# Weight transfers issued by POOL instead of the common queue, and POOL's small fills on VectorE, in a hybrid attention and mLSTM encoder layer

## Chip, cores and metric

One core of a Trainium2 chip runs the whole program. The metric is the device time of one execution in microseconds. Engines: PE is TensorE, DVE is VectorE, ACT is ScalarE, POOL is GpSimd, SP is SyncE. SP computes nothing in this kernel; it only issues transfers.

## What is computed

```python
def _encoder_layer(h, ...):                     # h: 16 meta tokens + sequence, 1024 wide
    xn = _rmsnorm(h, g_pre)
    proj = xn @ w_in + b_in                     # 1024 x 6672
    na_q, na_k, na_v, na_z, ml_qk, ml_v, ml_z, ml_o, ml_g, mg = jnp.split(proj, SPLIT_IDX, axis=-1)
    ya = _neighbourhood_attention(na_q, na_k, na_v, na_rpb)    # 8 heads of 64, window 8 x 16 on a grid 64 wide
    ya = (ya * jax.nn.silu(na_z)) @ w_a
    yb = (_mlstm_branch(ml_qk, ml_v, ml_g, ml_o, ml_conv_w, ml_head_g) * jax.nn.silu(ml_z)) @ w_b
    ga, gb = jnp.split(jax.nn.sigmoid(mg), 2, axis=-1)
    y = (ga * ya + gb * yb) @ w_out
    return h + _rmsnorm(y, g_post)
```

This is done once for a sequence of 1024 tokens (s = 0) and once for one of 2048 (s = 1), all in float32. The mLSTM branch has 4 heads of 128 and runs in both directions in chunks.

## The kernel before

Every float32 product is made of three products of a faster type: an operand x is split into `hi` (rounded) and `lo` (the rest), and `hi*hi + hi*lo + lo*hi` is added up in PSUM (`mm3`, lines 143 to 146, and the same by hand at 394 to 396 and 1284 to 1286).

Two generators run interleaved. `dense` makes the projections: `group` (input projections of 1024 tokens, by feature in `fm_half` and by token in `tm_unit`), then `final` for six blocks of 512 tokens. In `final` the first half multiplies `w_a` and `w_b` in 8 feature tiles (L144 to L146, with `yh`, `yl`); VectorE multiplies each result with a gate tile `tg` (L1263), adds the two branches (L1265) and splits them (L1266, L1267). The second half multiplies `w_out` in four column blocks (L1284 to L1286). `sparse` makes the mLSTM (`ml`, `ml_norm`) and neighbourhood attention (`na`) stages: scores (L644, L645), softmax (L648 to L661), transposition (L669) and splitting (L671, L672) of the weights, and the product with the values (L681). `run` takes from `dense` as much work as `sparse` has announced in us.

TensorE's order is written out by that interleaving. The order of all other engines, SP's and POOL's queues among them, is made by a scheduler when the program is built; each engine then works through its list in that order, so that an instruction that waits holds up all that follow on its engine. All transfers but 14 stand in SP's list.

The weights pass through `wload` and `wpump`. The first time that a tile of weights is used, it is loaded raw (`wraw`, L215), ScalarE makes `whi` (L233), POOL (the first three) or VectorE makes `wlo` (L236), and both are stored to memory (`wh`, `wl`, L240). Each later time they are loaded back from there (L231). Of `whi` and `wlo` there are four buffers each (`NBW = 4`); `wdone` is called where the last product of a tile has been issued to TensorE, and it pumps the next one:

```python
    def wdone(self, n=1):
        self.wout -= n
        self.wpump()
```

The gate tiles are loaded two feature tiles ahead, from four buffers (L1247):

```python
                    tg = fp.tile([P, n], F32, name="tg", tag="stT", bufs=4)
                    nc.sync.dma_start(tg, self.GT[s][8 * br + ft][:, t0:t0 + n])
```

POOL has little: the first three `wlo`, small fills of constants (`ss` L276, `km` L341 with two copies L342 and L343, `gt` L543 and L544, `g_t` L704 and L705, `g_mp` L760, `raw` L820 and L822, `va` L856 and L857, `st` L952), and the 14 transfers of `qB` (L541) and `kx` (L617) for attention.

Of the kernel before, what the change touches and what calls it, by code (L numbers as in the profile page):

```python
# [9 lines left out]
F32 = mybir.dt.float32  # L10
# [11 lines left out]
NM = 16  # L22
# [88 lines left out]
class K:  # L111
# [107 lines left out]
    def wpump(self):  # L219


        nc, wp = self.nc, self.wp
        self.wload()
        while self.wraw and self.wout < NBW:
            key, raw, nk, w = self.wraw.popleft()
            n = nk * w
            hi = wp.tile([P, 4 * WU], F32R, name="whi", bufs=NBW)
            lo = wp.tile([P, 4 * WU], F32R, name="wlo", bufs=NBW)
            if raw is None:
                for x, d in zip((hi, lo), self.wkept[key]):  # L230
                    nc.sync.dma_start(x[:, :n].bitcast(F32), d[:, :])  # L231
            else:
                nc.scalar.activation(hi[:, :n], raw[:, :n], AF.Copy)  # L233
                self.nu += 1
                eng = nc.vector if self.nu > 4 else nc.gpsimd
                eng.tensor_tensor(lo[:, :n], raw[:, :n], hi[:, :n].bitcast(F32), op=ALU.subtract)  # L236
                self.wkept[key] = []
                for x, part in ((hi, "h"), (lo, "l")):
                    d = self.dp.tile([P, n], F32, name=f"w{part}{len(self.wkept)}")
                    nc.sync.dma_start(d[:, :], x[:, :n].bitcast(F32))  # L240
                    self.wkept[key].append(d)
            self.wrdy.append([x[:, :n].rearrange("p (k c) -> p k c", k=nk) for x in (hi, lo)])
            self.wout += 1
            self.wload()
# [10 lines left out]
    def build_half(self, s, t0, meta, res, tags=("pj",), xp=None, per=4):  # L255

        nc, wp = self.nc, self.wp
        src = self.i["x_prompt" if s == 0 else "x_sample"]
        base = NM if meta else 0
        jobs = [(src[t0 + P * j:t0 + P * (j + 1), :], P, base + P * j) for j in range(4)]  # L260
        js = [jobs[a:a + per] for a in range(0, 4, per)]
        if meta:
            js[-1] = js[-1] + [(self.i["meta"], NM, 0)]
        xh = xl = None
        cnt = 0
        scaled = []
        for grp in js:
            xs = []
            for ap, n, col in grp:
                xr = (xp or wp).tile([P, D], F32, name="xr", bufs=5 if xp else 4)  # L270
                nc.sync.dma_start(xr[:n], ap)
                xs.append((xr, n, col))
            yield
            m = len(grp)
            ss = wp.tile([P, 5], F32, name="ss", bufs=2)
            nc.gpsimd.memset(ss, 1.0)  # L276
            for q, (xr, n, _) in enumerate(xs):
                junk = wp.tile([P, D], mybir.dt.bfloat16, name="xsq", tag="thT", bufs=1)
                nc.scalar.activation(junk[:n], xr[:n], AF.Square, accum_out=ss[:n, q:q + 1])
                yield  # L280
            nc.vector.tensor_scalar(ss[:, :m], ss[:, :m], 1.0 / D, EPS, op0=ALU.mult, op1=ALU.add)
            r = self.rsqrt8(wp, ss[:, :m], [P, m])
            yield
            for q, (xr, n, col) in enumerate(xs):
                nc.vector.scalar_tensor_tensor(xr[:n], xr[:n], r[:n, q:q + 1], self.gpre[:n], op0=ALU.mult, op1=ALU.mult)
                yield
            yield "scaled"
            if xh is None:
                xh = wp.tile([P, KT, HALF], F32R, name="xh", bufs=2)
                xl = wp.tile([P, KT, HALF], F32R, name="xl", bufs=2)  # L290
            for xr, n, col in xs:
                for e in range(2):
                    pt = self.psum(tags[cnt % len(tags)], [P, 4, P])
                    cnt += 1
                    for j in range(4):
                        nc.tensor.transpose(pt[:, j, :n], xr[:n, (4 * e + j) * P:(4 * e + j + 1) * P], self.ident[:n, :n])
                    h = xh[:, 4 * e:4 * e + 4, col:col + n]
                    nc.scalar.activation(h, pt[:, :, :n], AF.Copy)
                    nc.vector.tensor_tensor(xl[:, 4 * e:4 * e + 4, col:col + n], pt[:, :, :n], h.bitcast(F32), op=ALU.subtract)  # L299
                    yield  # L300
        res.append((xh, xl))


    def fm_evac(self, col, s, t0, meta, chunks, ps):

        nc, wp = self.nc, self.wp
        bi = (col // P) if col < 4608 else 36 + (col - 4624) // P
        bias = self.bfm[:, bi:bi + 1]
        st = wp.tile([P, HALF], F32, name="st", bufs=4)
        m = NM if meta else 0  # L310
        n = 512 + m
        for (c0, c1), p in zip(chunks, ps):
            o, q = st[:, c0:c1], p[:, :c1 - c0]
            if col < C_NK:
                nc.scalar.activation(o.rearrange("p (b r c) -> p r b c", r=8, b=4), q.rearrange("p (r b c) -> p r b c", r=8, b=4),
                                     AF.Identity, bias=self.bq8[:, bi:bi + 1], scale=0.125)
            elif C_NZ <= col < C_MQ:
                zb = wp.tile([P, HALF], F32, name="st", bufs=4)
                nc.scalar.activation(zb[:, c0:c1], q, AF.Identity, bias=bias)
                nc.scalar.activation(o, q, AF.Tanh, bias=self.bfh[:, bi:bi + 1], scale=0.5)  # L320
                nc.vector.scalar_tensor_tensor(o, o, 1.0, zb[:, c0:c1], op0=ALU.add, op1=ALU.mult)
            elif col >= C_GA:
                nc.scalar.activation(o, q, AF.Tanh, bias=self.bfh[:, bi:bi + 1], scale=0.5)
            else:
                nc.scalar.activation(o, q, AF.Identity, bias=bias)
        if C_MQ <= col < C_MV:
            dst = (self.MQ if col < C_MK else self.MK)
            h = (col % 512) // P
            lo = 0 if meta else NM + t0
            nc.sync.dma_start(dst[s][h][:, lo:lo + n], st[:, :n])  # L330
            if meta:
                nc.sync.dma_start(dst[1 - s][h][:, :NM], st[:, :NM])
            return
        if col >= C_GA:
            dst = self.GT[s][(col - C_GA) // P]
        else:
            dst = (self.NQ, self.NK, None, self.NZ)[col // 512][s][(col % 512) // P]
        nc.sync.dma_start(dst[:, t0:t0 + 512], st[:, m:n])
        if meta and C_NK <= col < C_NV:
            km = wp.tile([P, 64], F32, name="km", bufs=1)  # L340
            nc.gpsimd.memset(km, 0.0)  # L341
            nc.gpsimd.tensor_copy(km[:, 8:24], st[:, :NM])  # L342
            nc.gpsimd.tensor_copy(km[:, 32:48], st[:, :NM])  # L343
            nc.sync.dma_start(self.NKM[(col % 512) // P][:, :], km)

    def fm_half(self, col, w, x, s, t0, meta, done=None):
# [185 lines left out]
    def na(self, s, rts):  # L532
# [3 lines left out]
        with tc.tile_pool(name=f"na{s}{rts[0]}", bufs=1, side="right", reuse_waits="tile") as np_:  # L536
# [3 lines left out]
            for q in self.qB:  # L540
                nc.gpsimd.dma_start(q[64:128], i["onehot"].rearrange("a (b c) -> a b c", b=4))  # L541
            for g in self.gts:
                nc.gpsimd.memset(g[:, 0, :], 0.0)  # L543
                nc.gpsimd.memset(g[:, 16, :], 0.0)  # L544
            heads = [(rt, pr, hh) for rt in rts for pr in range(4) for hh in range(2)]
            n = len(heads)
            prep = self.na_prep(np_, s, rows, heads, 0)
# [147 lines left out]
    def ml_gates(self, s, keep, mp, res):  # L695
# [5 lines left out]
        kt = lambda n: keep.tile([P, NC_, 4], F32, name=n, bufs=1)  # L701
        gt = t("g_t", [P, NC_, 16])
        for d in range(2):
            nc.gpsimd.memset(gt[:, 0, 8 * d:8 * d + 4], -BIG)  # L704
            nc.gpsimd.memset(gt[:, 0, 8 * d + 4:8 * d + 8], 1.0e4)  # L705
        nc.sync.dma_start(gt[:NM, 0, :], self.GA[s][0:NM, :])
        nc.sync.dma_start(gt[:, 1:, :], self.GA[s][NM:, :].rearrange("(c p) g -> p c g", p=P))
        yield 3.0
# [21 lines left out]
        def one(d):  # L730
# [26 lines left out]
            nc.vector.tensor_tensor(ra, px[0:1, :NR], rg, op=ALU.add)  # L757
            me = t("g_me", [1, NR], bufs=2)
            mpv = t("g_mp", [1, NR], bufs=2)
            nc.gpsimd.memset(mpv, 0.0)  # L760
            yield
            for h in range(4):
                w = slice(h, NR, 4)
# [49 lines left out]
    def conv_load(self, mp, src, c0, n, T):  # L813

        nc = self.nc
        L = NM + T
        raw = mp.tile([P, BL + 2], F32, name="raw", bufs=3)
        a, b = max(c0 - 1, 0), min(c0 + n + 1, L)
        if a > c0 - 1:
            nc.gpsimd.memset(raw[:, 0:1], 0.0)  # L820
        if b < c0 + n + 1:
            nc.gpsimd.memset(raw[:, n + 1:n + 2], 0.0)  # L822
        nc.sync.dma_start(raw[:, a - c0 + 1:b - c0 + 1], src[:, a:b])
        return raw

# [14 lines left out]
    def ml(self, s):  # L840
# [3 lines left out]
        with tc.tile_pool(name=f"mg{s}", bufs=1, side="right", reuse_waits="tile") as keep:  # L844
# [8 lines left out]
            with tc.tile_pool(name=f"ml{s}", bufs=1, side="right", reuse_waits="tile") as mp:  # L853
                self.vas = [mp.tile([P, CB, 130], F32, name=f"va{j}") for j in range(3)]
                for va in self.vas:
                    nc.gpsimd.memset(va[:, :, 128:129], 1.0)  # L856
                    nc.gpsimd.memset(va[:, :, 129:130], 0.0)  # L857
                for h in range(4):
                    sts = {}
                    yield from self.ml_states(mp, s, h, g, NB, sts)  # L860
# [12 lines left out]
    def ml_states(self, mp, s, h, g, NB, sts):  # L873
# [51 lines left out]
        for i in range(N):  # L925
# [23 lines left out]
            b = (c0 - NM) // BL  # L949
            if b == NB - 1:  # L950
                sts[b] = mp.tile([P, CB, 260], F32, name="st", bufs=NB)
                nc.gpsimd.memset(sts[b][:, CB - 1, 130:260], 0.0)  # L952
            if b:
                sts[b - 1] = mp.tile([P, CB, 260], F32, name="st", bufs=NB)
            for j in range(CB - 1, -1, -1):
# [513 lines left out]
```

## Time and profile before

| | |
|---|---|
| median of 3 runs | 2958.22 us (2955.35 to 2959.94) |
| profiled execution | 2951.54 us, span 2949.8 us, granted clock 0.991 |
| PE, PEld | 2837.0 us (96%), 2520.4 us (85%) |
| DVE, ACT, POOL | 1788.2 us (61%), 1322.5 us (45%), 23.5 us (1%) |
| transfers | 633.33 MB, mean 215 GB/s; queue q1 (SP) 627.46 MB, queue q0 (POOL) 2.69 MB |

The profile is of one execution. A line such as `DVE tg L1263 <- DMA tg<-gt: 30.6, 21, 4.3` in a list of waits says that VectorE's instructions of line 1263 that write `tg` waited 30.6 us in total, 21 times and 4.3 us at most, for the transfer into `tg`. `SPq` is SP's queue of issues. In a list of groups the columns are line, engine, operation, tile written and tiles read, shapes and count; then busy us and mean ns of one; then the engine's idle time before them and what ended it. A row of the chain or of a timeline has start and length in us. The idle time of an engine that is not the bottleneck costs nothing.

### The profile page before, as it was taken

Reading aid. Unit: us, or ns where it says so; the run is one execution under the profiler, and the core shown is the slowest. Engines: PE = TensorE matmul, PEld = TensorE weight load, DVE = VectorE, ACT = ScalarE, POOL = GpSimd, SP = SyncE. Lnnn points to the kernel's source line nnn. Section 1 sums busy time; section 2 is a strip of 40 time slices with the busy share of each in tenths; the row PEclk is TensorE's granted clock in tenths of the full one; section 3 lists DMA queues with packets and bytes.
Section 4 is the critical chain, followed back from the end, with each engine's and each line's share of the span. In section 5 each row is a group of like instructions: output and inputs, shape, how many; then the busy total and the mean of one; then the engine's idle time right before and its main releaser. Section 6 shows DMA issues by size and latency. Waiting matters only on the chain. (4 is left out here: it accounts for less than half of the span.)

```text
span 2949.8 us, 49769 instructions
## 1 busy us (share of the span) xinstructions
PE 2837.0 (96%) x17616; PEld 2520.4 (85%) x17616; DVE 1788.2 (61%) x4818; ACT 1322.5 (45%) x3178; POOL 23.5 (1%) x111
## 2 busy tenths in 40 slices
PE   6999999999999999999999999999999989999998
PEld 6998897899799988888888988877887978888897
DVE  5233566556656764565566565495568877776853
ACT  4113545433443453455565454434455544544421
POOL 1000000000000000000000000000000000000000
PEclk9999999999999999999999999999999999999999
DMA  7555666556756563666765554496579898988875
GB/s 252 199 176 183 204 212 204 166 176 210 237 176 197 152 189 101 203 193 194 222 206 189 173 182 151 160 356 196 179 232 329 288 276 268 281 273 252 287 260 205
DMA packets 415914, 633.33 MB, mean 215 GB/s; under 512 B 51920, under 2 KB 252704, under 8 KB 415664
## 3 DMA queue, kind: packets, MB, share of 16 engines
q1 hardware_dynamic: 414544, 627.46, 66.7%
q0 software_dynamic: 1120, 2.69, 0.4%
q8 instruction: 138, 2.26, 0.3%
q14 instruction: 112, 0.92, 0.1%
HBM read 438.27 MB, written 191.74 MB: 214 GB/s over the span
## 5 line engine op out<-in xcount | busy, mean ns | idle before, releaser
L144 PE MATMUL pj<-xh,whi 128*128 128x512 f32 (+1 forms) x1824 | 722.4, 396 | 1.2 <-DVE xl L299 0.9
L145 PE MATMUL pj<-xl,whi 128*128 128x512 f32 (+1 forms) x1824 | 701.9, 385 | 0.1
L146 PE MATMUL pj<-xh,wlo 128*128 128x512 f32 (+1 forms) x1824 | 700.2, 384 | 0.0
L394 PE MATMUL pj<-whi,xh 128*128 128x256 f32 (+3 forms) x1576 | 450.9, 286 | 0.0
L395 PE MATMUL pj<-wlo,xh 128*128 128x256 f32 (+3 forms) x1576 | 444.6, 282 | 0.0
L396 PE MATMUL pj<-whi,xl 128*128 128x256 f32 (+3 forms) x1576 | 444.0, 282 | 0.0
L146 PEld LDWEIGHTS pj<-xh,wlo 128*128 128x128 f32 x1824 | 345.2, 189 | 72.3
L144 PEld LDWEIGHTS pj<-xh,whi 128*128 128x128 f32 x1824 | 345.9, 190 | 57.6 <-DVE xl L299 1.3
L145 PEld LDWEIGHTS pj<-xl,whi 128*128 128x128 f32 x1824 | 346.1, 190 | 53.7 <-DVE xl L299 0.4
L394 PEld LDWEIGHTS pj<-whi,xh 128*128 128x128 f32 (+1 forms) x1576 | 294.1, 187 | 1.2
L395 PEld LDWEIGHTS pj<-wlo,xh 128*128 128x128 f32 (+1 forms) x1576 | 293.8, 186 | 1.1
L396 PEld LDWEIGHTS pj<-whi,xl 128*128 128x128 f32 (+1 forms) x1576 | 293.9, 186 | 0.9
L1284 PE MATMUL pj<-whi,mh 128*128 128x256 f32 x768 | 220.1, 287 | 0.6 <-DVE yo L1312 0.6
L652 ACT ACTIVATE prb<-sc,mx 128x384 f32<-128x384 f32 (+2 forms) x192 | 119.5, 622 | 220.1 <-DVE mx L648 211.4
L1286 PE MATMUL pj<-whi,mlo 128*128 128x256 f32 x768 | 216.4, 282 | 0.0
L1285 PE MATMUL pj<-wlo,mh 128*128 128x256 f32 x768 | 216.2, 281 | 0.0
L672 DVE TENSOR_TENSOR pts<-tr,pts 96x512 fp32r<-96x512 f32 (+2 forms) x192 | 131.9, 687 | 120.6 <-ACT pts L671 119.6
L671 ACT ACTIVATE pts<-tr 96x512 fp32r<-96x512 f32 (+2 forms) x192 | 114.5, 596 | 153.2 <-PE tr L669 152.3
L144 PE MATMUL pj<-yh,whi 128*128 128x512 f32 x384 | 158.0, 411 | 19.8 <-DVE tg L1263 19.8
L403 DVE TENSOR_TENSOR stT<-pj,bb 128x256 f32<-128x256 f32 (+3 forms) x197 | 83.0, 422 | 123.5 <-PE pj L396 121.7
L146 PE MATMUL pj<-yh,wlo 128*128 128x512 f32 x384 | 153.0, 398 | 0.0
L145 PE MATMUL pj<-yl,whi 128*128 128x512 f32 x384 | 152.8, 398 | 0.0
(234 smaller groups left out, 5145.0 us busy)
## 6 DMA issues: line engine op xcount, KB each, us to landing
whi<-wh SPq DMA_DIRECT2D x176, 512.0 KB
wlo<-wl SPq DMA_DIRECT2D x176, 512.0 KB
wh<-whi SPq DMA_DIRECT2D x64, 512.0 KB
wl<-wlo SPq DMA_DIRECT2D x64, 512.0 KB
wraw<-w_in SPq DMA_DIRECT2D x48, 512.0 KB
gt<-st SPq DMA_DIRECT2D x96, 256.0 KB
tg<-gt SPq DMA_DIRECT2D x96, 256.0 KB
xr<-x_sample SPq DMA_DIRECT2D x24, 512.0 KB
```

What stands on the lines that cost most here:

```text
L144: mm(out, ah, bh, start=start, stop=False)
L145: mm(out, ah, bl, start=False, stop=False)
L146: mm(out, al, bh, start=False, stop=stop)
L394: nc.tensor.matmul(o, xh, wh, start=k == 0, stop=False)
L395: nc.tensor.matmul(o, xh, wl, start=False, stop=False)
L396: nc.tensor.matmul(o, xl, wh, start=False, stop=k == KT - 1)
L652: nc.scalar.activation(pr_[:, :N].rearrange("p (b a c) -> p b a c", b=4, c=8), sc[:, :N].rearrange("p (a b c) -> p b a c", b=4, c=8), AF.E ...
L671: nc.scalar.activation(pts[:ks, :, 0, :], pt[:ks], AF.Copy)
L672: nc.vector.tensor_tensor(pts[:ks, :, 1, :], pt[:ks], pts[:ks, :, 0, :].bitcast(F32), op=ALU.subtract)
L1284: nc.tensor.matmul(o, mh[:, k, xs], wh, start=k == 0, stop=False)
L1285: nc.tensor.matmul(o, mh[:, k, xs], wl, start=False, stop=False)
L1286: nc.tensor.matmul(o, ml[:, k, xs], wh, start=False, stop=k == KT - 1)
```

## The change

The loads and stores of split weights are issued on POOL's queue instead of SP's, and the small fills and copies that POOL made are made by VectorE. The first three `wlo` and the transfers of `qB` and `kx` stay with POOL.

```diff
@@ wpump
                 for x, d in zip((hi, lo), self.wkept[key]):
-                    nc.sync.dma_start(x[:, :n].bitcast(F32), d[:, :])
+                    nc.gpsimd.dma_start(x[:, :n].bitcast(F32), d[:, :])
...
-                    nc.sync.dma_start(d[:, :], x[:, :n].bitcast(F32))
+                    nc.gpsimd.dma_start(d[:, :], x[:, :n].bitcast(F32))
@@ build_half
-            nc.gpsimd.memset(ss, 1.0)
+            nc.vector.memset(ss, 1.0)
@@ fm_evac
-            nc.gpsimd.memset(km, 0.0)
-            nc.gpsimd.tensor_copy(km[:, 8:24], st[:, :NM])
-            nc.gpsimd.tensor_copy(km[:, 32:48], st[:, :NM])
+            nc.vector.memset(km, 0.0)
+            nc.vector.tensor_copy(km[:, 8:24], st[:, :NM])
+            nc.vector.tensor_copy(km[:, 32:48], st[:, :NM])
@@ na
-                nc.gpsimd.memset(g[:, 0, :], 0.0)
-                nc.gpsimd.memset(g[:, 16, :], 0.0)
+                nc.vector.memset(g[:, 0, :], 0.0)
+                nc.vector.memset(g[:, 16, :], 0.0)
...
```

In the same way the fills at L704, L705, L760, L820, L822, L856, L857 and L952 go from `nc.gpsimd` to `nc.vector`.

More of the change, by code (lines that the diff above doesn't have):

```diff
@@ L703, in ml_gates @@
         for d in range(2):
-            nc.gpsimd.memset(gt[:, 0, 8 * d:8 * d + 4], -BIG)
-            nc.gpsimd.memset(gt[:, 0, 8 * d + 4:8 * d + 8], 1.0e4)
+            nc.vector.memset(gt[:, 0, 8 * d:8 * d + 4], -BIG)
+            nc.vector.memset(gt[:, 0, 8 * d + 4:8 * d + 8], 1.0e4)
         nc.sync.dma_start(gt[:NM, 0, :], self.GA[s][0:NM, :])
@@ L759, in one @@
             mpv = t("g_mp", [1, NR], bufs=2)
-            nc.gpsimd.memset(mpv, 0.0)
+            nc.vector.memset(mpv, 0.0)
             yield
@@ L819, in conv_load @@
         if a > c0 - 1:
-            nc.gpsimd.memset(raw[:, 0:1], 0.0)
+            nc.vector.memset(raw[:, 0:1], 0.0)
         if b < c0 + n + 1:
-            nc.gpsimd.memset(raw[:, n + 1:n + 2], 0.0)
+            nc.vector.memset(raw[:, n + 1:n + 2], 0.0)
         nc.sync.dma_start(raw[:, a - c0 + 1:b - c0 + 1], src[:, a:b])
@@ L855, in ml @@
                 for va in self.vas:
-                    nc.gpsimd.memset(va[:, :, 128:129], 1.0)
-                    nc.gpsimd.memset(va[:, :, 129:130], 0.0)
+                    nc.vector.memset(va[:, :, 128:129], 1.0)
+                    nc.vector.memset(va[:, :, 129:130], 0.0)
                 for h in range(4):
@@ L951, in ml_states @@
                 sts[b] = mp.tile([P, CB, 260], F32, name="st", bufs=NB)
-                nc.gpsimd.memset(sts[b][:, CB - 1, 130:260], 0.0)
+                nc.vector.memset(sts[b][:, CB - 1, 130:260], 0.0)
             if b:
```

## The prediction

> **What bounds the kernel now.** I read first the page's busy shares and slices, then the busy time by stage, then the waits of each engine in the stage that stands out, and last the queue order at one of its stalls. The page and its issue list:
>
> ```profile
> PE 2837.0 (96%) x17616; PEld 2520.4 (85%) x17616; DVE 1788.2 (61%) x4818; ACT 1322.5 (45%) x3178; POOL 23.5 (1%) x111
> ...
> whi<-wh SPq DMA_DIRECT2D x176, 512.0 KB
> wlo<-wl SPq DMA_DIRECT2D x176, 512.0 KB
> wh<-whi SPq DMA_DIRECT2D x64, 512.0 KB
> wl<-wlo SPq DMA_DIRECT2D x64, 512.0 KB
> ...
> tg<-gt SPq DMA_DIRECT2D x96, 256.0 KB
> ```
>
> TensorE is busy 96% of 2949.8 us, and its program order is the same before and after. All that any change of queues can win is therefore in the 113 us in which TensorE idles (2949.8 - 2837.0). The same subtraction by stage (columns: stretch, its length, then busy time of PE, PEld, DVE, ACT, POOL, then granted clock, DMA share, GB/s):
>
> ```profile
> 0.00:2200.00 2200.00, 2138.99 (x13143) 1896.10 (x13144) 1248.08 (x3547) 999.37 (x2401) 22.50 (x109) 0.99 0.62 195
> 2200.00:2850.00 650.00, 610.38 (x3912) 545.13 (x3911) 494.71 (x1151) 310.56 (x738) 1.02 (x2) 0.99 0.87 277
> 2850.00:2949.80 99.80, 87.65 (x564) 79.12 (x563) 45.45 (x121) 12.56 (x40) 0.00 (x0) 0.97 0.68 245
> ```
>
> The first 2200 us lose 61 us (2.8%), the stage from 2200 to 2850, where the final projections run beside neighbourhood attention, loses 40 us (6.1%), and the tail 12 us. The late stage is also the one with the DMA engines at 0.87. Its waits, of TensorE, of VectorE and of SyncE's queue (total us, times, longest):
>
> ```profile
> PE sm L681 <- DVE pts L672: 19.8, 20, 2.6
> PE pj L144 <- DVE tg L1263: 17.4, 5, 5.4
> ```
>
> ```profile
> DVE tg L1263 <- DMA tg<-gt: 30.6, 21, 4.3
> ```
>
> ```profile
> SPq L231 <- PE pj L1286: 85.0, 23, 11.8
> SPq L231 <- PE pj L146: 32.1, 15, 6.2
> ```
>
> So 37.2 of the 40 us go through VectorE, and VectorE sits 30.6 us there waiting for the gate tiles tg to land; no row has TensorE waiting for a weight. SyncE's queue meanwhile stands 117.1 us (85.0 + 32.1) at L231: the next weight load is at its head and its buffer is not free yet, and everything issued behind it stands too. One stall closely, in the chain of waits and in the queue's timeline (start, time, what):
>
> ```profile
> 2383.95 0.33 SPq L231 DMA_DIRECT2D whi<-wh  x1
> 2384.96 0.33 SPq L231 DMA_DIRECT2D wlo<-wl  x1
> ...
> 2385.63 10.82 DMA tg<-gt
> 2396.45 0.02 issue
> 2396.47 0.70 DVE tg L1263
> 2397.17 0.04 issue
> 2397.21 0.80 PE pj L144
> ```
>
> ```profile
> 2397.21 0.80 PE L144 MATMUL pj<-yh,whi 128*128 128x512 f32 x1 [5.37 <-DVE tg L1263]
> ```
>
> A tg issued right behind a pair of weight loads took 10.82 us to land and cost TensorE 5.37 us. The weights ahead of it were in no hurry:
>
> ```profile
> L1284 PE MATMUL pj<-whi,mh x768: 274/282/388, 2276.9 to 2939.5; 128*128 128x256 f32 x192
> ...
> L144 PE MATMUL pj<-yh,whi x384: 387/395/796, 2212.8 to 2893.5; 128*128 128x512 f32 x192
> ```
>
> L144 uses a weight tile 8 times and L1284 16 times, so these are 48 + 48 tiles in 2939.5 - 2212.8 = 727 us: one pair per 7.6 us. With four buffers a load has about three tiles, 23 us, before it is used.
>
> **Part 1, the weight loads (L231) leave SyncE's queue for POOL's.** Beside the rows above the issue list has the wider ones:
>
> ```profile
> whi<-wh SPq DMA_DIRECT2D x8, 528.0 KB
> ...
> wh<-whi SPq DMA_DIRECT2D x4, 528.0 KB
> ```
>
> Removed from SP: 2 x 184 loads (176 and 8) and 2 x 68 stores (64 and 4), 504 issues. The built order confirms it: SP's rows fall from 2086 to 1564, POOL's rise from 107 to 533. What POOL pays for an issue, and how long such a transfer takes, stands in the 14 that it issues already:
>
> ```profile
> L617 POOL DMA_DIRECT2D kx<-masks x10 | 5.1, 517 | 898.4 <-PE sc L645 898.2 <-issue 0.2
> ```
>
> ```profile
> kx<-masks POOLq DMA_DIRECT2D x4, 208.0 KB, 7.6
> ...
> kx<-masks POOLq DMA_DIRECT2D x4, 192.0 KB, 3.2
> ```
>
> 517 ns each on 64 partitions; a weight has 128, so I take between 0.5 and 1.0 us: 504 issues are 250 to 500 us on an engine that was busy 23.5 us. Landing takes 3.2 us in quiet places and 7.6 us in crowded ones for 0.2 MB. A weight of 0.5 MB that took twice the worse value, 15 us, would still be inside the 23 us of lead. Cost on TensorE: 0; if that cover is gone, every us beyond 23 is paid once per pair.
>
> The gain is what stood behind the weights. A pair is 1.05 MB, at the stage's 277 GB/s 3.8 us of transfer that a following tg no longer sits behind, and the queue no longer stands 117.1 us. The bound above is all 17.4 us of L144's waits; the bound below is a loss, since the bytes are the same and the weights still take their share of the same engines (priced as a rival). I take half, 8.7 us, because in those 10.82 us the weights were about half of what was queued. L681's 19.8 us are nearer to TensorE's own chain (transposes, ScalarE, VectorE), and only the part in which VectorE was held up at a tg goes; I take a fifth, 4.0 us. What is late next is the pts step L672 itself, which stays.
>
> In the first 2200 us the largest of TensorE's 61 us is at the very start, where x is loaded and normalised:
>
> ```profile
> PE pj L296 <- DVE xr L285: 22.4, 2, 18.0
> ```
>
> There I take 0, between a loss of 2 us and a gain of 2 us, since no wait in TensorE's list names a transfer.
>
> **Part 2, the stores (L240).** They move past SP's loads of x and of raw weights. A store is waited for only by the next owner of its whi or wlo buffer, three tiles later, and by the first reload, hundreds of us later. 0 us. At the start POOL also makes the first three lo halves (L236), and stores now stand between them:
>
> ```profile
> L236 POOL TENSOR_TENSOR wlo<-wraw,whi 128x1024 fp32r<-128x1024 f32 x3 | 7.0, 2349 | 12.5 <-ACT whi L233 12.4
> ```
>
> An issue of at most 1 us between subtractions of 2.3 us, with 12.5 us idle before them: 0, at most 1 us.
>
> **Part 3, POOL's queue gets waits in it.** qB (L541) and kx (L617) now stand behind weight loads. At the start of the first attention stage the order puts the two qB and two kx behind a pair that was issued at:
>
> ```profile
> 773.37 0.40 SPq L231 DMA_DIRECT2D whi<-wh  x1
> 773.87 0.40 SPq L231 DMA_DIRECT2D wlo<-wl  x1
> ```
>
> ```profile
> 786.66 0.69 PE L645 MATMUL sc<-kx,qB 128*128 128x384 f32 x1 [0.54 <-DVE kx L626]
> ```
>
> Four issues of 0.5 us end at 776.4 and land 3.2 to 7.6 us later, by 784; L645 needs them at 786.7. Hidden, by 2.7 us at worst; without that cover 0 to 5 us, once or twice.
>
> **Part 4, 87 fills and copies on VectorE.** Nearest rows: 99 to 208 ns on POOL, 159 ns for one of VectorE's smallest operations.
>
> ```profile
> L660 DVE RECIPROCAL sm<-sm 128x1 f32<-128x1 f32 x192 | 30.6, 159 | 77.1 <-ACT prb L652 76.6
> ```
>
> ```profile
> L952 POOL MEMSET st<- 128x130 f32 x8 | 1.7, 208 | 154.1 <-DVE ccl L1039 154.1
> L822 POOL MEMSET raw<- 128x1 f32 x16 | 1.6, 99 | 377.9 <-DVE cv L835 222.2 <-ACT hb L1089 141.1 <-DMA kf<-kf 7.3
> ...
> L341 POOL MEMSET km<- 128x64 f32 x4 | 0.6, 152 | 7.2 <-DMA nkm<-km 7.2
> ```
>
> 87 x 0.1 to 0.2 us = 9 to 17 us of VectorE, nearly all before 2200, where it is idle 952 us (2200 - 1248). New is that VectorE may stand at L341 until the previous nkm store has landed, 7.2 us over four times, with pts and stT queued behind. I take 2 us on TensorE, between 0 and 7.
>
> **The sum.** -8.7 - 4.0 + 0 + 0 + 2.0 = -10.7 us. The profiled execution took 2951.5 us (span 2949.8 and 1.7 around it), so 2940.8; the median of the three runs, 2958.2, lies 6.7 above it, so the forecast is 2947.5 us.
>
> **A rule against the trace.** The profile's row has a transfer from POOL's queue at 7.6 us in crowded places, no shorter than what SP's tg takes there. The Trainium skill (DMA: Bandwidth & Descriptors, section "Issuing engines are not separate DMA queues") says that transfers from several engines run on the same 16 DMA engines and that a second issuer saves only issue time; by that rule the sum would have no 8.7 and no 4.0, and come out at +2. No run here separates the two yet.
>
> **Rivals.**
>
> *The engines are the limit, not the queue: no change.* For it: DMA share 0.87 and 277 GB/s between 2200 and 2850, and the 7.6 us of kx. Against: 117.1 us in which SP stood at L231. Time: 2951.5 + 2 + 6.7 = 2960 us. This is the case of the rule just cited.
>
> *Weights overtake the gates: slower.* In one queue a weight behind a tg waits for it. In two queues the engines serve both, and if they alternate by rows, a weight row is 4 KB (1024 f32, the L236 row above) and a tg row 2 KB (512 f32):
>
> ```profile
> L1263 DVE SCALAR_TENSOR_TENSOR tg<-tg,pj 128x512 f32<-128x512 f32 x96 | 65.5, 684 | 50.3 <-DMA tg<-gt 44.2 <-PE pj L146 5.4
> ```
>
> Weights then get two thirds while both are queued. A tg pair (0.52 MB) then moves at 92 GB/s instead of 277: 5.7 us, not 1.9, so 3.8 us later. VectorE waited for a tg 21 times in that stage, where there is no slack left: 21 x 3.8 = 80 us of VectorE, of which TensorE saw 17.4/30.6, 57%: 45 us; half of it, since a pair of 1.05 MB at 185 GB/s is gone after 5.7 of 7.6 us and tg then has all: 23 us. Time: 2951.5 + 23 + 6.7 = 2981 us. It decides once tg lands later than about 11 us (10.82 cost 5.37 us). For it: weights have 23 us of slack and tg none, so first come first served is the better order. Against: SP issues tg earlier when it isn't standing at L231. The Trainium skill (the same page, "Queues, rings and completion order") has each engine take turns between queues packet by packet, which is this mechanism.
>
> *VectorE starves POOL's descriptor writing: slower.* The place would be L661, VectorE's scaling, which POOL's issues meet on the attention stages:
>
> ```profile
> L661 DVE TENSOR_SCALAR prb<-prb,sm 128x512 f32<-128x512 f32 (+2 forms) x97 | 45.1, 465 | 1.9
> ```
>
> It is 45.1 us of 650 in pieces of 0.47 us; one piece delays one load by that much, and it decides only past 23 us of lead. If pairs were 1 us late beyond it, 80 us in the late stage: 3038 us. The Trainium skill (SBUF — State Buffer, section "SBUF: two separate sides") warns of just this for transfers issued by POOL; no run here shows it so far.
>
> **How the numbers follow.** Sum as worked out: 0.44. Engines the limit: 0.18. Weights overtake: 0.30. Starved, or POOL's or VectorE's queue blocked for longer than priced: 0.08. A change of 0.2%, 6 us, is about what a measurement of this kernel can tell from none. So faster 0.44, same 0.18, slower 0.38. The likeliest case's own range is 2930 (L144's waits all gone, 17.4, and half of L681's, 9.9: 2931) to 2952. The whole range goes on to the overtaking case with a little over it, 2985: above it are starvation and the worst of overtaking (0.13), below 2930 some 0.05.
>
> **What would show it.** Right: SP has no waits for PE at L231 and POOL's queue has them; VectorE's wait for tg falls from 30.6 us to about 15, L144's from 17.4 to about 9, TensorE's idle between 2200 and 2850 from 40 to about 27, and no TensorE wait names whi or wlo. Overtaking: tg landings of 11 us and more, VectorE's wait for tg over 50 us, L144's over 30. Starvation: TensorE waits for whi or wlo. No change: the same waits to within 5 us. Part 4 is wrong if VectorE waits over 7 us at L341 with TensorE idle beside it. The forecast is wrong as a whole if the first 2200 us change by over 6 us, for then the rescheduled order, which I price at 0, decides.

## The result and the profile after

The changed kernel takes 2980.22 us (median of 4 runs, 2978.66 to 2987.07), the kernel before 2957.06 us beside it (median of 4): ratio 1.0082, 95% interval 1.0064 to 1.0100. It is 23 us slower where 10.7 us of gain were forecast. The profiled execution took 2979.81 us, span 2978.0.

The page of the changed kernel, its busy line and its list of transfers (median us from issue to landing last):

```profile
PE 2844.4 (96%) x17616; PEld 2527.0 (85%) x17616; DVE 1791.4 (60%) x4905; ACT 1323.7 (44%) x3178; POOL 286.6 (10%) x528
...
whi<-wh POOLq DMA_DIRECT2D x176, 512.0 KB, 5.8
wlo<-wl POOLq DMA_DIRECT2D x176, 512.0 KB, 6.3
```

TensorE's idle time goes from 112.8 us to 2978.0 - 2844.4 = 133.6 us, 20.8 us more: that is most of the 28.2 us between the two profiled spans (2978.0 - 2949.8). The same stretches as in the prediction's table, cut where TensorE has come equally far in its program (2200 before is 2235.9 here, 2850 is about 2877):

```profile
0.00:2235.90 2235.90, 2151.06 (x13143) 1904.48 (x13144) 1250.58 (x3634) 1000.21 (x2401) 183.03 (x337) 0.99 0.61 192
2235.90:2877.70 641.80, 606.75 (x3918) 544.52 (x3917) 496.41 (x1156) 310.94 (x738) 90.74 (x167) 0.99 0.87 281
2877.70:2978.00 100.30, 86.62 (x559) 77.98 (x557) 44.46 (x117) 12.56 (x40) 12.87 (x24) 0.97 0.66 240
```

Idle by stretch is 84.8, 35.1 and 13.7 us, where it was 61.0, 39.6 and 12.2. The late stage, for which the change was costed, gained 4.6 us. The first 2200 us, costed at nothing, lost 23.8. (TensorE's busy time there also grew, by 12.1 us, 2151.06 against 2138.99 for the same 13143 matmuls; the granted clock of the two profiled executions is 0.987 and 0.991. I judge by idle time and by the ratios of timed runs, not by that.)

TensorE's waits over the whole span (total us, times, longest):

```profile
...
PE sm L681 <- DVE pts L672: 18.9, 16, 2.4
PE pj L144 <- DVE tg L1263: 11.4, 8, 2.9
PE tr L669 <- DVE prb L661: 10.6, 5, 4.2
PE tr L1184 <- DVE hn L1173: 10.1, 1, 10.1
PE sc L644 <- ACT prb L652: 8.9, 4, 4.0
...
PE sc L644 <- ACT kd L624: 5.6, 1, 5.6
PE pj L144 <- ACT xh L298: 5.5, 1, 5.5
```

Added up by row over the first stretch, TensorE's waits grow from 60.7 to 84.6 us. The largest growths are 7.7 us at the start (L144 behind L298, and L145 behind L299), 7.5 at L1184, where TensorE waits for the normalised rows, 7.2 at L644, where it begins the attention's scores, and 3.5 at L144 behind L1003 in the mLSTM's scan. Two places of the loss follow, and then one that shows why the late stage gained so little.

**At the start**, the chain of waits, ScalarE's and TensorE's timeline:

```profile
19.19 12.96 DMA wraw<-w_in
```

```profile
32.17 1.06 ACT L233 ACTIVATE whi<-wraw 128x1024 fp32r<-128x1024 f32 x1 [4.53 <-DMA wraw<-w_in]
```

```profile
36.29 0.59 PE L144 MATMUL pj<-xh,whi 128*128 128x264 f32 x1 [5.54 <-ACT xh L298]
```

ScalarE's list now has the split of the third weight (L233) ahead of four splits of x (L298). The weight's raw load takes 12.96 us, and ScalarE stands 4.53 us with x ready behind it. In the kernel before, the same split came after those of x and waited for nothing:

```profile
30.77 1.05 ACT L233 ACTIVATE whi<-wraw 128x1024 fp32r<-128x1024 f32 x1
```

**At the first normalisation**, the chain of waits and VectorE's timeline:

```profile
732.46 10.82 DMA tog<-to
...
743.99 0.08 DVE nwt L133
...
748.85 0.61 DVE hn L1173
...
749.80 0.66 PE tr L1184 x2
```

```profile
743.30 0.69 DVE L1158 SCALAR_TENSOR_TENSOR hn<-tog,hn 128x512 f32<-128x512 f32 x1 [4.16 <-DMA tog<-to]
```

VectorE stands 4.16 us at an L1158, and the Newton steps (L133 to L135) of an earlier pair, for whose L1173 TensorE waits, stand behind it. In the kernel before, this L1158, the sixth, came after that L1173, and waited for nothing; the fifth was the last one ahead of it:

```profile
727.82 0.69 DVE L1158 SCALAR_TENSOR_TENSOR hn<-tog,hn 128x512 f32<-128x512 f32 x1 [0.17 <-DMA tog<-to]
...
735.30 1.28 DVE L1173 TENSOR_TENSOR hn<-hn,szg 128x512 f32<-128x512 f32 x2
...
736.92 0.68 DVE L1158 SCALAR_TENSOR_TENSOR hn<-tog,hn 128x512 f32<-128x512 f32 x1
```

The late tog is not new by itself. Before, the sixth tog was issued at 727.07, right behind four weight loads in SP's own queue (723.76 to 726.46), and VectorE came to its L1158 9.85 us later. Here it is issued at 732.46 between four weight loads of POOL's queue (731.46 to 733.41), and VectorE comes to it 6.7 us later (743.30 - 4.16), before it has landed.

**In the late stage**, the chain of waits:

```profile
2522.39 10.51 DMA tg<-gt
...
2532.92 0.04 DVE tg L1263
...
2533.80 0.61 DVE sc L648
...
2535.01 0.41 DVE prb L661
...
2535.56 0.45 PE tr L669
```

The same picture: tg lands 10.51 us after its issue, and L648 and L661 stand behind the L1263 that needs it. TensorE waits for L661 at L669.

### The profile page after: what moved, and what is told of

It is laid out like the page before. It is cut to its first block, busy times and chain, and to the rows that moved or that the text cites. A ratio compares the mean times of both kernels' runs of the same rounds, so it can differ in the third digit from the quotient of the medians.

```text
span 2978.0 us, 49720 instructions
## 1 busy us (share of the span) xinstructions
PE 2844.4 (96%) x17616; PEld 2527.0 (85%) x17616; DVE 1791.4 (60%) x4905; ACT 1323.7 (44%) x3178; POOL 286.6 (10%) x528
## 4 chain that ended last, share of the span: by engine, by line
PE 76%; DMA 12%; DVE 7%; ACT 2%; issue 2%; SPq 1%; DVEq 0%; ACTq 0%
PE pj L144 13%; PE pj L145 12%; PE pj L146 12%; PE pj L394 6%; PE pj L395 6%; PE pj L396 6%; DMA tg<-gt 3%; PE pj L1284 3%; PE pj L1286 3%; PE pj L1285 3%; PE sm L681 2%; PE tr L669 2%; DMA um<-ud 2%; PE sm L146 1%; PE sc L644 1%
## 5 line engine op out<-in xcount | busy, mean ns | idle before, releaser
L144 PE MATMUL pj<-xh,whi 128*128 128x512 f32 (+1 forms) x1824 | 726.1, 398 | 6.4 <-ACT xh L298 5.5
L145 PE MATMUL pj<-xl,whi 128*128 128x512 f32 (+1 forms) x1824 | 705.2, 387 | 2.2 <-DVE xl L299 2.2
L144 PEld LDWEIGHTS pj<-xh,whi 128*128 128x128 f32 x1824 | 348.2, 191 | 63.6 <-ACT xh L298 5.6
L145 PEld LDWEIGHTS pj<-xl,whi 128*128 128x128 f32 x1824 | 348.3, 191 | 56.2 <-DVE xl L299 2.5
L231 POOL DMA_DIRECT2D whi<-wh x184 | 100.5, 546 | 1232.1 <-PE pj L146 1100.8
L652 ACT ACTIVATE prb<-sc,mx 128x384 f32<-128x384 f32 (+2 forms) x192 | 119.5, 623 | 220.2 <-DVE mx L648 211.3
L671 ACT ACTIVATE pts<-tr 96x512 fp32r<-96x512 f32 (+2 forms) x192 | 114.5, 596 | 158.8 <-PE tr L669 157.9
L144 PE MATMUL pj<-yh,whi 128*128 128x512 f32 x384 | 157.1, 409 | 11.4 <-DVE tg L1263 11.4
L231 POOL DMA_DIRECT2D wlo<-wl x184 | 100.0, 543 | 666.5 <-PE pj L396 363.7
```

Source lines behind the costliest of these rows:

```text
L144: mm(out, ah, bh, start=start, stop=False)
L145: mm(out, ah, bl, start=False, stop=False)
L231: nc.gpsimd.dma_start(x[:, :n].bitcast(F32), d[:, :])
L652: nc.scalar.activation(pr_[:, :N].rearrange("p (b a c) -> p b a c", b=4, c=8), sc[:, :N].rearrange("p (a b c) -> p b a c", b=4, c=8), AF.E ...
```

## The experiments

Ratios are to the kernel before, measured beside each kernel; idle is span minus TensorE's busy time of the one profiled execution (before 112.8 us, changed kernel 133.6).

| kernel | median us, before beside it | ratio, 95% interval | idle us |
|---|---|---|---|
| fills alone | 2955.88, 2955.55 | 1.0003, 0.9990 to 1.0017 | 2953.3 - 2843.8 = 109.5 |
| loads alone | 2971.26, 2955.55 | 1.0053, 1.0035 to 1.0071 | 2964.6 - 2842.0 = 122.6 |
| stores alone | 2970.76, 2955.55 | 1.0053, 1.0032 to 1.0074 | 2968.9 - 2850.0 = 118.9 |
| late loads alone | 2952.20, 2955.55 | 0.9988, 0.9975 to 1.0001 | 2952.8 - 2841.3 = 111.5 |
| loads, order held | 2963.78, 2957.30 | 1.0020, 1.0005 to 1.0035 | 2965.6 - 2850.6 = 115.0 |
| stores, first four on SP | 2957.56, 2957.30 | 1.0006, 0.9996 to 1.0017 | 2954.5 - 2840.0 = 114.5 |
| gates on POOL | 2948.03, 2957.30 | 0.9975, 0.9964 to 0.9987 | 2947.2 - 2841.4 = 105.8 |
| gates, L1150, fills | 2954.56, 2957.30 | 0.9996, 0.9981 to 1.0010 | 2950.6 - 2843.1 = 107.5 |
| changed, both repairs | 2968.68, 2957.01 | 1.0045, 1.0028 to 1.0061 | 2976.1 - 2853.3 = 122.8 |
| gates, order held | 2948.31, 2957.01 | 0.9972, 0.9952 to 0.9992 | 2952.1 - 2848.5 = 103.6 |
| gates, late weights | 2953.14, 2957.01 | 0.9980, 0.9965 to 0.9995 | 2951.8 - 2842.8 = 109.0 |
| gates, yr, xres | 2943.64, 2957.01 | 0.9951, 0.9935 to 0.9968 | 2946.1 - 2839.4 = 106.7 |
| both repairs, wide weights on SP | 2965.91, 2954.76 | 1.0032, 1.0017 to 1.0048 | 2963.2 - 2842.9 = 120.3 |
| gates, yr, xres, qr, kr | 2938.53, 2954.76 | 0.9931, 0.9909 to 0.9954 | 2936.5 - 2840.0 = 96.5 |
| gates, yr, xres, um | 2948.53, 2954.76 | 0.9984, 0.9966 to 1.0002 | 2946.4 - 2842.2 = 104.2 |

### The change in parts

Fills alone: the fills of the change, queues as before.

> Only the 87 fills and copies go to VectorE; loads and stores of weights stay on SP. Theory A (the loss comes from the transfers: weights that no longer stand in SP's line compete with the loads that a new stage waits for): 2957 us, at most 3 us off, since nothing of the queues changes. Rival B (the fills and the order that is rebuilt around them cost the time): most of the 23 us are here, 2972 to 2980 us. The prediction's part 4: plus 2 us, 0 to 7.

Loads alone:

```diff
-                    nc.sync.dma_start(x[:, :n].bitcast(F32), d[:, :])
+                    nc.gpsimd.dma_start(x[:, :n].bitcast(F32), d[:, :])
```

> Only the loads L231 go to POOL; stores stay on SP, fills on POOL. Theory A: the 8.3 us lost in the first 100 us go away if the four stores between SP's first loads caused them, the 11.6 us at 700 to 800 and the some 15 us at 1000 to 2200 stay, the late stage gains some 8: 2957 + 36 - 8 - 8 = 2977 at most, 2966 to 2977 us. Rival B (fills): no slower than before, 2945 to 2957 us. Rival C (stores): the loss is gone altogether, 2949 us.

Stores alone:

```diff
-                    nc.sync.dma_start(d[:, :], x[:, :n].bitcast(F32))
+                    nc.gpsimd.dma_start(d[:, :], x[:, :n].bitcast(F32))
```

> Only the stores L240 go to POOL; loads stay on SP, fills on POOL. Theory A: the 8.3 us at the start, and nothing at 700 to 800, where no weight is stored for the first time in the changed kernel's jump: 2963 to 2967 us. Rival C (stores cause the loss everywhere): 2972 us and more. Prediction's part 2: 0 to plus 1 us.

Late loads alone:

```diff
-                    nc.sync.dma_start(x[:, :n].bitcast(F32), d[:, :])
+                    (nc.sync if key[0] == "i" else nc.gpsimd).dma_start(x[:, :n].bitcast(F32), d[:, :])
```

> Loads L231 of w_a, w_b and w_out alone (the late stage) go to POOL; those of w_in, the stores and the fills stay where they were. Theory A: the first 2200 us as before, within 2 us, and the late stage gains what it gained in the changed kernel, 7.6 us: 2947 to 2953 us. Rival D (the late gain was only slack that the delay ahead of it had made, loads that arrive earlier because TensorE is late): no gain, 2955 to 2960 us.

The fills cost nothing; rival B falls. Loads and stores each lose about 0.5%, so rival C falls as well. TensorE's waits with the stores alone, in the first 100 us, and then with the loads alone, between 700 and 820:

```profile
PE pj L144 <- ACT xh L298: 5.2, 1, 5.2
```

```profile
PE tr L1184 <- DVE hn L1173: 9.2, 1, 9.2
PE sc L644 <- ACT prb L652: 6.4, 2, 4.0
```

So the start belongs to the stores and the normalisation to the loads. The stores alone took more than theory A had expected (2971, not 2963 to 2967). With four runs that size is uncertain: their idle time is 118.9, 6.1 us more than before, which is nearer to theory A. The late loads alone come to 2952, inside their range, but their interval takes in 1, and the trace says why it is so little. TensorE's waits from 2200 to 2850, in the kernel before and then with the late loads alone:

```profile
PE tr L669 <- DVE prb L661: 0.5, 2, 0.3
```

```profile
PE sm L681 <- DVE pts L672: 21.7, 16, 2.8
PE tr L669 <- DVE prb L661: 10.8, 5, 3.9
PE pj L144 <- DVE tg L1263: 4.7, 4, 2.1
```

L144's wait falls from 17.4 us to 4.7, and L669's rises from 0.5 to 10.8: the wait for tg has only moved to another of TensorE's instructions.

### Order or transfer

Loads, order held: L1158 reads its constant 1.0 from a tile of one column (the cell), which is computed from the normalised pair two before. So VectorE's list can't have L1158 ahead of that pair's L1173.

```diff
-                nc.vector.scalar_tensor_tensor(hb, to, 1.0, hb, op0=ALU.add, op1=ALU.mult)
+                nc.vector.scalar_tensor_tensor(hb, to, one[i - 2] if i >= 2 else 1.0, hb, op0=ALU.add, op1=ALU.mult)
...
+            if e == 0: one[i] = mp.tile([P, 1], F32, name="one", bufs=3); nc.vector.tensor_scalar(one[i], hb[:, 0, 0:1], 0.0, 1.0, op0=ALU.mult, op1=ALU.add)
```

> Loads L231 on POOL as in the experiment with loads alone (2971 us), and one thing about the order: L1158 of a pair of rows takes its 1.0 from a cell that is computed from the normalised pair two before it, so that the order written at build time can't put it ahead of that pair's L133 to L1173. The queues and what they carry stay. Theory A1 (a late tog costs time because VectorE's list has L1158 ahead of work that TensorE waits for): TensorE's wait at its first L1184 goes from 9.2 us back to about 5, the 12.6 us of the stretch 700 to 800 fall by 4 to 8, and the stretch 1900 to 2000 gets some of its 6.1 back: 2959 to 2967 us. Theory A2 (the transfers come late and that alone decides, whatever the order): unchanged, 2969 to 2973 us.

Stores, first four on SP:

```diff
-                    nc.gpsimd.dma_start(d[:, :], x[:, :n].bitcast(F32))
+                    (nc.gpsimd if self.nu > 3 else nc.sync).dma_start(d[:, :], x[:, :n].bitcast(F32))
```

> Stores L240 on POOL as in the experiment with stores alone (2971 us), but the first four, those of the first two weights, stay on SP. Theory A: these four let SP run ahead, so that the third weight's raw load is planned early and ScalarE's list gets its split ahead of the splits of x; with them on SP the 7.4 us of the first 100 us go, 2962 to 2965 us, and TensorE has no wait of 5 us for xh near 36 us. Rival: some other store is behind it, 2969 to 2973 us. What the other stores cost between 1100 and 1700, some 7 us, stays in either case.

TensorE's waits between 700 and 820 with the order held, and in the first 100 us with four stores back:

```profile
PE sc L644 <- ACT prb L652: 5.6, 2, 2.9
PE tr L1184 <- DVE hn L1173: 3.7, 1, 3.7
```

```profile
PE pj L144 <- ACT xh L298: 0.2, 1, 0.2
```

With the same queues and only L1158 held back, the 9.2 us at L1184 become 3.7, and the ratio goes from 1.0053 to 1.0020 (the two intervals only touch): theory A1. With the first four of 136 stores back on SP the stores' loss is gone (1.0053 to 1.0006, intervals apart), and so is the wait at the start: there A is shown, to the place. The time is lower than A's 2962 to 2965. Of the 13 us between the two medians, the idle times account for 4.4 (118.9 - 114.5); the rest lies in TensorE's busy time, so the size is uncertain. What doesn't go with the order held is the other row: L644's wait for prb was 6.4 us and is 5.6. ScalarE's timeline of that kernel:

```profile
803.61 0.84 ACT L624 ACTIVATE kd<-kr 128x768 fp32r<-128x768 f32 x1 [4.64 <-DMA kr<-nkm]
```

Before, L624 had no wait at this place, and the pair of weight loads there went out 3.7 us behind kr (795.79 and 792.09). Here the pair is issued at 791.66, ahead of kr at 794.21. ScalarE stands 4.64 us for kr, with L652 behind it.

### Both repairs in the changed kernel

> The changed kernel (2980 us) with the two repairs found so far: the first four stores back on SP, and the cell that holds L1158 behind the normalisation. Theory A (separate causes that add up): 2980 less 13.2 (stores alone 2970.8 to 2957.6) less 7.5 (loads alone 2971.3 to 2963.8) is 2959 us, 2955 to 2964. Rival: something that only loads and stores together cause is still there, 2968 to 2978 us. A part of some 8 us at the starts of the attention stages, where kr, gt and qr land later beside the weights, has to stay in either case, so not below 2953.

2969 us: the repairs do not add up to 2959, and the rival's range holds. Of the changed kernel's 0.82% the two repairs take back 0.37 (1.0082 to 1.0045). One of the places left is an overtaking by weights. POOL's and SP's timelines, the chain and TensorE of this kernel:

```profile
1694.12 0.54 POOL L231 DMA_DIRECT2D wlo<-wl  x1 [27.21 <-PE pj L396]
1694.66 0.54 POOL L231 DMA_DIRECT2D whi<-wh  x1
1695.54 0.55 POOL L231 DMA_DIRECT2D wlo<-wl  x1 [0.34 <-PE pj L396]
1696.08 0.54 POOL L231 DMA_DIRECT2D whi<-wh  x1
```

```profile
1694.75 0.91 SPq L985 DMA_DIRECT2D um<-ud  x2
```

```profile
1695.24 9.64 DMA um<-ud
```

```profile
1706.55 0.47 PE L144 MATMUL sc<-qh,kh 128*128 128x128 f32 x1 [5.92 <-ACT qh L1003]
```

And SP's and VectorE's timelines of the same place before:

```profile
1680.18 0.90 SPq L985 DMA_DIRECT2D um<-ud  x2
...
1682.49 0.41 SPq L231 DMA_DIRECT2D whi<-wh  x1
```

```profile
1684.21 0.43 DVE L1023 TENSOR_TENSOR um<-um,trim 128x256 f32<-128x256 f32 x1 [3.18 <-DMA um<-ud]
```

Before, the two um went out 2.3 us ahead of the weights, and the first was used 4.0 us after its issue (1684.21 - 1680.18). Now the second um is issued in the middle of four weight loads (2 MB) and takes 9.64 us. TensorE waits for qh (L1003), which needs no um: in ScalarE's list it stands behind L1025, which does, as it did before. In the changed kernel without the repairs TensorE's wait for qh here is 2.3 us. The test of the overtaking puts the four loads back on SP:

```diff
-                    nc.gpsimd.dma_start(x[:, :n].bitcast(F32), d[:, :])
+                    (nc.sync if key[0] == "i" and w != P else nc.gpsimd).dma_start(x[:, :n].bitcast(F32), d[:, :])
```

> The changed kernel with the two repairs (2969 us), and the loads of the weights that are 256 and 264 columns wide (released by L396, in bursts of four) back on SP; the 128-column weights, w_a, w_b and w_out stay on POOL. Theory T (weights overtake um): um beside them lands in 4 us again, TensorE's wait of 5.9 us for qh near 1700 is gone, 1600 to 1700 gets some 6 us back: 2955 to 2963 us. Rival (order, or TensorE's clock in that one profile): um's landing doesn't decide, 2966 to 2972 us.

Between 1600 and 1800 TensorE then has no wait in its list, where it had 5.9 us. But the median moves only from 2969 to 2966, between theory T's range and the rival's, and the intervals overlap: the mechanism is shown in the trace, its share of the time is not. The kernel is still slower than before, by 0.32%. Waits that are left stand at the attention's first blocks; TensorE's waits between 700 and 820 in this kernel:

```profile
PE sc L644 <- ACT kd L624: 5.6, 1, 5.6
PE sc L644 <- ACT prb L652: 4.1, 2, 2.4
```

The two rows at L644 were 3.8 and 0.2 us before. The rows of the attention are loaded there beside 128-column weights, which are still on POOL. No run takes this place alone, so whether it is all of the rest stays open.

### The other way round: short loads on POOL

Gates on POOL, with weights, stores and fills as before:

```diff
-                    nc.sync.dma_start(tg, self.GT[s][8 * br + ft][:, t0:t0 + n])
+                    nc.gpsimd.dma_start(tg, self.GT[s][8 * br + ft][:, t0:t0 + n])
```

> The kernel before, with the gate loads L1247 (tg) alone on POOL; weights, stores and fills stay. The mirror of the change: now the short transfer that VectorE stands on has a queue for itself. Theory A (a queue of its own gets its share of the engines at once, and what matters is whether the transfer in it is the one that is waited for): tg lands in 3 to 5 us, not some 7.5, VectorE's tg wait falls from 44 us to under 15, TensorE's waits at L144 behind it from 17 to under 5, 2940 to 2947 us. Rival E (the 16 engines are full there, and tg takes what it takes): tg's landing unchanged, 2955 to 2959 us. Rival F (the order written anew puts other work behind tg, as in the changed kernel): tg's waits gone, but L669 waits for L661 by some 8 us: 2947 to 2953 us.

VectorE's group of L1263 in this kernel:

```profile
L1263 DVE SCALAR_TENSOR_TENSOR tg<-tg,pj 128x512 f32<-128x512 f32 x96 | 64.8, 681 | 17.4 <-DMA tg<-gt 8.8 <-PE pj L146 7.1 <-PE sc L645 0.5
```

and its list of transfers:

```profile
tg<-gt POOLq DMA_DIRECT2D x96, 256.0 KB, 6.6
```

VectorE's wait for tg falls from 44.2 us to 8.8 and the kernel is faster, 0.9975. The time, 2948, lies just above theory A's range and inside rival F's, but F's sign is not there: L669 waits 0.2 us for L661 between 2200 and 2850. A is wrong in one part: tg takes 6.6 us to land, not 3 to 5. What is seen is an earlier issue. From the issue of a tg to the L1263 that reads it the trace has 10.7 us (median of 96), where it was 8.1 before: tg no longer stands behind a weight load that waits for its buffer at the head of SP's queue.

With the 72 loads of L1150 on POOL as well, and the fills on VectorE:

> As the experiment with the gates on POOL, and besides the 72 loads L1150 (hn, tog, szg) on POOL and the fills on VectorE. Theory A: TensorE's waits at L1184 for L1173 (5.3 and 2.8 us, two normalisations) halve: 3 to 5 us below the gates alone, 2936 to 2944 us. Rival: 72 issues of 0.5 us in POOL's order, each behind the buffer it waits for, come later than on SP (0.43 us each), and the weights behind them on SP arrive later: no better than the gates alone, or up to 5 us worse.

Nothing is left of the gain (0.9996), a little worse than the rival had it. From 739.80 to 748.39 TensorE stands 8.59 us at an L1184, a wait that the profile puts down to nothing; why is open. The control for the cell, on the gates alone:

> The gates on POOL (2948 us) with the cell that holds L1158 behind the normalisation. It is also the control for that cell: if the cell saved time by itself, and not by undoing what the change did, this is 4 to 8 us faster than the gates alone, 2940 to 2944. If the cell only undoes the change's reordering: 2945 to 2951 us, at most the 1.5 us by which L1184's wait was shorter than before.

0.9972 beside 0.9975: the cell saves nothing by itself that these runs can tell; it undid what the change had done to the order. Then more on POOL beside the gates: the late weights (the edit of late loads alone); or the rows yr and xres, as below; or these and the rows qr and kr (`self.nc.gpsimd` at L530); or yr, xres and um (`nc.gpsimd` at L985):

```diff
-                nc.sync.dma_start(yr[k], ...
+                nc.gpsimd.dma_start(yr[k], ...
...
-                nc.sync.dma_start(x, src[todo[j][1], todo[j][2]])
+                nc.gpsimd.dma_start(x, src[todo[j][1], todo[j][2]])
```

> Gates and late weights (w_a, w_b, w_out) both on POOL, all else as before. Theory A (what counts is when a gate is issued and what shares the engines with it): gates stand behind weight pairs in one queue again, but no longer behind the attention rows; about as the better of the two, 2946 to 2953 us. Rival (two gains that add): 2940 to 2945 us. Rival (POOL's queue becomes what SP's was): tg waits of 30 us and more, 2953 to 2960 us.

> Gates, the rows yr (L1225) and the residual rows xres (L1337) on POOL, all else as before. Theory A: VectorE's waits for xres (about 1 us each at L1350 in the late stage) shrink as those for tg did: 2943 to 2948 us. Rival: more transfers of POOL's queue stand in one order, each behind its own buffer, so that gates wait behind yr: 2948 to 2956 us.

> Gates, yr and xres on POOL (2944 us), and with them the rows qr and kr of the attention (L530). Theory T turned round (a short load that an engine stands on belongs in the queue that isn't behind the weights): ScalarE's waits at L619 and L624 for qr and kr shrink, 2936 to 2942 us. Rival (everything short in one queue again, each behind the buffer it waits for; 4 issues of 0.5 us for each row block): 2944 to 2952 us.

> Gates, yr and xres on POOL (2944 us), and with them the masks um (L985) of the scans. Theory T turned round: TensorE waited little for um in the kernel before (3.2 us of VectorE near 1684, hidden), so 0 to 3 us less, 2940 to 2944 us. Rival: um now stands behind POOL's fills L822 in POOL's order, which wait for VectorE and ScalarE (up to 12 us of idle before one): 2946 to 2955 us.

Late weights beside the gates add nothing (2953, which is not told apart from the gates alone). The short rows do: 2944, and with qr and kr 2939 us, a ratio of 0.9931, the best kernel of the study and 16 us below before. Its late stage, the same matmuls as 2200 to 2850 before, and TensorE's largest waits in it:

```profile
2205.60:2839.70 634.10, 609.43 (x3912) 546.22 (x3911) 496.72 (x1153) 311.01 (x739) 157.60 (x290) 0.99 0.87 284
```

```profile
PE sm L681 <- DVE pts L672: 8.9, 11, 2.2
PE pj L144 <- DVE tg L1263: 7.2, 4, 2.3
PE sc L644 <- ACT prb L652: 6.0, 2, 5.2
```

Idle is 24.7 us (634.10 - 609.43) where it was 39.6. That is what the prediction had hoped of the change (27), from the same stall, by moving the other side of it. With um the gain shrinks to 2949, as its rival had it (the interval still meets that of 2944).

## Why the prediction was wrong

*The step that failed* is the 0 for the first 2200 us: "no wait in TensorE's list names a transfer". That list names only what released TensorE. L1184's 5.2 us were put down to VectorE, and one step behind VectorE stood tog, for which VectorE already waited, 0.17 us at the last L1158 ahead of it. The loads at the start of a stage had next to no slack, and a list of TensorE's waits can't show it. The prediction named this point itself ("the rescheduled order, which I price at 0, decides"). It was 23.8 us of idle time. At the start and at the normalisation, ScalarE's and VectorE's lists had an instruction that stands for a transfer ahead of work that TensorE needs, and the two repairs take these waits away or shorten them. At the attention's first blocks and at um the traces have late loads, and no run shows their share of the time.

*The late stage* was right in its two terms: L144 17.4 to 7.4 us (forecast -8.7, measured -10.0) and L681 19.8 to 16.1 (forecast -4.0, measured -3.7). But the stage gained 4.6 us and not 12.7. The missing term is L669 behind L661: 0.5 to 10.6 us, since VectorE now stands for tg with L661 behind. VectorE's wait for tg fell to 24.0 us there, not to 15:

```profile
DVE tg L1263 <- DMA tg<-gt: 24.0, 14, 3.8
```

*Stores at 0 to 1 us*: the prediction asked who waits for a store and whether POOL has time for it. The cost was on the other side: the stores had paced SP and the raw weight loads behind them. The first four cost some 8 us at the start: of the first 100 us TensorE idles 30.5 in the changed kernel, 22.4 before and 22.8 with those four back on SP.

*qB and kx behind weights, and the fills*: right. TensorE waits 0.4 us for kx. Fills alone are 1.0003, from which the 2 us can't be told.

*The count of issues*: the rows of the built order (2086 to 1564 on SP, 107 to 533 on POOL) differ by 522 and 426, so they don't confirm the 504. The traces do: SP issues 504 transfers fewer (2332 to 1828), and POOL has 417 instructions more (111 to 528), 504 less the 87 fills and copies. (A second slip changes nothing either: the 45.1 us of L661 are of 700 us, 2200 to 2900, not of 650.)

*Rivals.* "The engines are the limit" is out: by a choice of queues alone the best kernel is 16 us faster, and it moves 284 GB/s in the late stage, where it was 277, at the same share of 0.87. The Trainium skill (DMA: Bandwidth & Descriptors, "Issuing engines are not separate DMA queues") says that a second issuer only saves the time of issuing. The ratio of 0.9931 disagrees: SP's queue goes in order and stood 117.1 us at L231, and a transfer on another queue doesn't stand with it. "VectorE starves POOL" is out: POOL's issues of loads took 546 and 543 ns each in the changed kernel, the loads landed in 5.8 and 6.3 us, and TensorE waited for no whi or wlo. "Weights overtake the gates" has the time, 2981 us, but not the place: VectorE's wait for tg fell. So it is luck that its time fits, and that the range, which reached up to 2985 for its sake, takes in 2980. Its mechanism is seen elsewhere in the first 2200 us: um (9.64 us in the kernel with both repairs) and kr stand beside weights that used to go out behind them. The Trainium skill (the same page, "Queues, rings and completion order") has each engine take turns between queues. The 9.64 us of um among four weight loads agree.

## What to carry to other kernels

Call a transfer patient if nothing waits for it for a long time. Before a big, patient transfer leaves a shared queue, list the short loads that were issued ahead of or among it, and what each engine has behind the instruction that needs them. Their slack is in the waits of VectorE and ScalarE, not in TensorE's. If one queue stands on a patient transfer, move the short loads that are waited for, and leave the patient ones where they are. When instruction order is written at build time, moving a transfer also rewrites the lists of engines that the edit doesn't touch: compare them, and price a late load by what stands behind it.

## What the runs showed of the hardware

On POOL's queue a tg took 6.6 us to land (6.3 in the best kernel). The ten tg of SP's queue that stand in the chain of waits before took 6.7 to 10.8 us, and the profile has no landing time for the others. So it isn't shown that another queue moves a short transfer faster. What is shown is the earlier issue, 10.7 us ahead of the use and not 8.1. And POOL executed 528 instructions in the changed kernel, most of them issues of transfers of 0.54 us, beside a VectorE that was busy 60% of the time, at no cost that shows: VectorE was busy 1791.4 us, 1788.2 before, with 87 operations more.
